# Hybrid decoder layer, one core: other places for the SBUF tiles, other orders of units and column groups, another source for the first norm

## Chip, cores and metric

One Trainium2 chip, one of its cores. The metric is the device time of one execution in microseconds (us), as a median over runs.

## What is computed

One decoder layer on 256 tokens of width 2048, in float32: a combined input projection that feeds eight gated-DeltaNet heads and eight block-sparse attention heads, an output projection, a cross-attention over 256 memory tokens, a gated MLP with a causal convolution, and a final norm. Cut to what matters here:

```python
def hybrid_mixer(x, ...):
    h = rmsnorm(x, norm_g)
    proj = h @ w_in                        # q, k, v, z, b, a | q, k, v  (7184 columns)
    qkv_a = silu(causal_dwconv(qkv_a, gdn_conv_w))
    o_a = rmsnorm(gated_delta_rule(...), gdn_norm_g) * silu(z_a)
    o_b = rmsnorm(moba_attention(q_b, k_b, v_b, rel_bias), moba_norm_g)
    return concatenate([o_a, o_b]) @ w_out

def cross_attention(x, mem, ...):          # 4 heads, keys and values from mem
def conv_ffn(x, ...):
    h = rmsnorm(x, norm_g)
    gate = causal_dwconv(h @ w_gate, conv_w) + conv_b
    return (silu(gate) * (h @ w_up)) @ w_down

x = x + hybrid_mixer(x); x = x + cross_attention(x, mem); x = x + conv_ffn(x)
return rmsnorm(x, final_norm_g)
```

## The kernel before, in words

**Numbers in two parts.** Each float32 operand of a large matmul is a sum of two float32r parts. `split` writes the tokens as `xT[:, k, :512]`: 256 columns of high part and 256 of low part for each of the 16 row tiles k. Each weight unit (128 x up to 1024 numbers) arrives by DMA in `raw`, ScalarE copies it to `hi`, and VectorE writes the remainder to `lo` (`prep`, which handles one unit). Three products are summed: high weight times both parts of the tokens, and low weight times the high part.

**Units and blocks.** Two units make a pair, which one DMA of SyncE's queue brings (`load_pair`); the ring has three `raw` tiles, four `hi` and four `lo`. `w_block` computes 128 output columns, transposed, from two units with eight row tiles each (`w_unit`): in a unit first eight matmuls with a `hi` slice as the stationary operand and the 512 columns of `xT[:, k]` as the moving one, and then eight with a `lo` slice and 256 columns. Both units of a block go hi, lo, hi, lo; the job that empties the block's PSUM bank is added after the last low matmul. There are 152 such blocks: 40 in the input projection, 4 memory keys, 16 of the output projection, 4 cross-attention queries and 88 gate and up blocks of the MLP. `s_block` does it the other way round: a slice of tokens (or of `actT`) is stationary and 256 to 512 columns of `hi` or `lo` move; for a row tile and a half of the tokens there are three matmuls (high by `hi`, low by `hi`, high by `lo`). The z gate, the values and the whole down projection (`actT`, 22 row tiles a half) are made so.

**Order.** `stream` issues the units in the order of the list `units`; between the parts of a unit `jobs.tick` issues steps of generators (evacuations, the recurrence, attention, norms) by a planner that keeps estimated engine times. The planner sets only the order in which each engine's instructions stand in its queue. The list begins with the 400 columns of the first z group (`z_pairs(0)`, whose first 16 columns are the decay inputs b and a), the first two row tiles in a unit each and the others two in a unit; then eight K blocks, after each of which comes one pair of the second and third z groups (384 and 256 columns); then Q, value, V, attention blocks, output projection, cross-attention, MLP.

**The start.** `start_job` splits the row tiles of `xraw`, the channel-major tokens, as they land; `load_x` loads them between the first weight pairs. After row tile 11 it also loads the tokens a second time, as they are in memory (`xn`, four DMAs of 512 KB on SyncE's queue), and sums their squares on ScalarE for the first norm's factor `r1`. `z_evac` and the jobs that need `r1` wait for it. Nine warm-up matmuls on `ones` run before the first data.

**Places in SBUF.** Tiles of a pool lie one behind the other in the order in which they are made, each rounded up to 32 bytes a partition; the pool `p0` begins at byte 16512. From the sizes in the code follow these starts in a partition: `cst` 16512, `sml` (338 floats), `ones`, `pw`, `raw` 20480, `hi` 45056, `lo` 61440, `xT` 77824, the small tiles `t` 110592, the three `pad`, `stats`, the four `tt` 130656, `relb`, then the tag E (`xraw`, later the bias tables and the residual) at 138880 and behind it the pool `pm` from 155264 (the heads' tiles AB, later `mT`; `oTm`, `oTg`, `oTx`). Modulo 512 that is 0 for `raw`, `hi`, `lo`, `xT` and `t`, 96 for `tt`, 128 for E and for every tile of `pm`. The pool `pf` of the MLP replaces `pm` and starts with a filler of 96 floats, so `actT` lies at 155648, 0 modulo 512.

## Time and profile before

| | us |
|---|---|
| median of 3 runs (lowest, highest) | 1337.7 (1336.53, 1338.1) |
| the profiled execution, its own time | 1335.58 |
| its span, first to last instruction | 1333.8 |
| TensorE busy in the span | 1318.6 (99%) |
| VectorE, ScalarE, GpSimd busy | 935.2, 692.3, 54.6 |
| mean granted TensorE clock | 0.998 of 2.4 GHz |
| moved by DMA | 250.43 MB, 188 GB/s on average |

TensorE's busy time is made of matmuls that overlap: one matmul's listed duration (some 390 ns for 512 columns) is from its start to its end in the pipeline, and the pace is read from start to start. So a stretch in which TensorE is busy throughout is judged by its length over the number of its matmuls.

### The profile page before, as it was taken

What the parts mean: (1) busy time and instruction counts of PE and PEld (TensorE: products, weight loads), DVE (VectorE), ACT (ScalarE), POOL (GpSimd) and SP (SyncE); (2) the same over time, 40 slices, a digit from 0 to 9 for tenths busy, and PEclk for the clock granted to TensorE, in tenths of its full rate; (3) what the DMA queues carried; (4) which work ended last, traced back from release to release, by engine and by line L of the source; (5) the groups of instructions that cost most, each with busy time, mean ns of one, the idle gap of its engine ahead of it and who ended that gap; (6) DMA issues with size and microseconds to landing.
All of it is one profiled execution on the core that took longest, in us unless ns stands there. A gap on an engine that the chain in (4) does not pass through costs nothing.

```text
span 1333.8 us, 19353 instructions
## 1 busy us (share of the span) xinstructions
PE 1318.6 (99%) x7414; PEld 1149.5 (86%) x7414; DVE 935.2 (70%) x1594; ACT 692.3 (52%) x1114; POOL 54.6 (4%) x140
## 2 busy tenths in 40 slices
PE   8999999999999999999999999999999999999997
PEld 8998888888788889998888888888888888888886
DVE  5688889867686766687777777545577777775554
ACT  5776555567564544565544445434344454444443
POOL 0101000202110000000000000000000000000000
PEclk9999999999999999999999999999999999999999
DMA  9665655624255655454545555555555555555552
GB/s 342 227 236 197 219 178 186 205 92 147 103 190 184 235 190 190 137 212 160 188 167 187 188 189 189 199 197 199 189 190 189 190 190 190 189 190 189 190 189 95
DMA packets 50793, 250.43 MB, mean 188 GB/s; under 512 B 11603, under 2 KB 15884, under 8 KB 23436
## 3 DMA queue, kind: packets, MB, share of 16 engines
q1 hardware_dynamic: 49152, 245.53, 51.6%
q0 software_dynamic: 448, 2.11, 0.5%
q10 hardware_dynamic: 1100, 1.54, 0.3%
q8 instruction: 58, 0.95, 0.3%
q14 instruction: 35, 0.29, 0.1%
HBM read 246.53 MB, written 2.64 MB: 187 GB/s over the span
## 4 chain that ended last, share of the span: by engine, by line
PE 68%; issue 0%; DVE 0%; ACT 0%; POOLq 0%; POOL 0%; ACTq 0%; DVEq 0%
PE bank L96 68%; ACT xn L96 0%; DVE tt L96 0%; DVE xT L96 0%; DVE xn L96 0%; POOLq L1462 0%; POOL stats L96 0%; DVE oTx L96 0%; DVE lo L96 0%; ACT oTx L96 0%; ACTq L96 0%; DVE xres L96 0%; DVE stats L96 0%; DVEq L96 0%
## 5 line engine op out<-in xcount | busy, mean ns | idle before, releaser
L96 DVE TENSOR_TENSOR lo<-raw,hi 128x1024 fp32r<-128x1024 f32 (+4 forms) x449 | 540.3, 1205 | 321.0 <-ACT hi L96 316.1
L96 ACT ACTIVATE hi<-raw 128x1024 fp32r<-128x1024 f32 (+4 forms) x449 | 466.8, 1041 | 431.4 <-PE bank L96 331.0
L96 PE MATMUL bank<-xT,hi 128*128 128x512 f32 x2112 | 542.9, 396 | 1.4 <-DVE xT L96 1.4
L96 PEld LDWEIGHTS bank<-xT,hi 128*128 128x128 f32 x2112 | 377.5, 189 | 70.4 <-issue 2.6
L96 PEld LDWEIGHTS bank<-xT,lo 128*128 128x128 f32 x2112 | 288.1, 190 | 20.0 <-issue 0.6
L96 PE MATMUL bank<-xT,lo 128*128 128x256 f32 x2112 | 301.1, 284 | 0.0
L96 PE MATMUL bank<-hi,actT 128*128 128x512 f32 x704 | 216.8, 389 | 0.0
L96 PEld LDWEIGHTS bank<-hi,actT 128*128 128x128 f32 x704 | 132.0, 188 | 27.2
L96 PE MATMUL bank<-lo,actT 128*128 128x512 f32 x352 | 136.9, 389 | 0.0
L96 PE MATMUL bank<-hi,xT 128*128 128x512 f32 (+3 forms) x320 | 86.1, 353 | 3.3 <-ACT xT L96 2.4
L96 DVE SCALAR_TENSOR_TENSOR t<-pad,sml,t 128x256 f32<-128x256 f32 x160 | 78.2, 489 | 7.8
L96 PEld LDWEIGHTS bank<-lo,actT 128*128 128x128 f32 x352 | 66.1, 188 | 13.8
L96 ACT ACTIVATE t<-bank 128x256 f32<-128x256 f32 (+1 forms) x164 | 56.8, 349 | 25.9 <-PE bank L96 25.9
L96 PEld LDWEIGHTS bank<-hi,xT 128*128 128x128 f32 x320 | 56.9, 190 | 8.8 <-ACT xT L96 3.2
L96 DVE TENSOR_TENSOR t<-bank,t 128x256 f32<-128x256 f32 x132 | 55.1, 417 | 9.7 <-ACT t L96 9.6
L96 PE MATMUL bank<-lo,xT 128*128 128x512 f32 (+3 forms) x160 | 55.9, 349 | 0.0
L96 POOL TENSOR_TENSOR stats<-stats,pw 128x2 f32<-128x2 f32 (+1 forms) x38 | 28.9, 761 | 564.0 <-DVE stats L96 564.0
L96 ACT ACTIVATE t<-t,sml 128x256 f32<-128x256 f32 x44 | 22.3, 506 | 39.6 <-DVE t L96 38.9
L96 DVE TENSOR_TENSOR t<-t,t 128x256 f32<-128x256 f32 x96 | 41.0, 428 | 2.0
L96 ACT ACTIVATE actT<-t 128x256 fp32r<-128x256 f32 x44 | 18.0, 413 | 46.6 <-DVE t L96 46.6
L96 PEld LDWEIGHTS bank<-lo,xT 128*128 128x128 f32 x160 | 30.3, 190 | 2.6
L96 PE MATMUL bank<-oTg,hi 128*128 128x512 f32 x128 | 32.4, 395 | 0.0
(157 smaller groups left out, 992.6 us busy)
## 6 DMA issues: line engine op xcount, KB each, us to landing
raw<-wst SPq DMA_DIRECT2D x212, 1024.0 KB, 4.8
raw<-wz SPq DMA_DIRECT2D x4, 768.0 KB, 4.1
raw<-wz SPq DMA_DIRECT2D x3, 800.0 KB, 8.3
xn<-x SPq DMA_DIRECT2D x4, 512.0 KB, 8.6
raw<-wz SPq DMA_DIRECT2D x4, 512.0 KB, 4.2
tt<-mem SPq DMA_DIRECT2D x8, 256.0 KB, 5.2
tt<-memT SPq DMA_DIRECT2D x8, 256.0 KB, 5.1
xres<-xT SPq DMA_DIRECT2D x4, 512.0 KB, 5.7
```

The costliest lines, as they stand in the source:

```text
L96: r = f(o, *a, **k)
```

## The change

It does five things.

- **Places.** `sml` loses the MLP's convolution numbers (162 floats instead of 338); they become a tile `smf` of `pf`, loaded by GpSimd's queue ahead of `fg`. `stats` has 516 floats instead of 640 (the scratch of `decay_job` is now in a `t` tile), a filler of 4 floats follows it, and `pf` has no filler.
- **Turned second units.** With `turn`, a unit goes low first and then high, and its last high matmul ends the block. All second units of input projection, cross-attention queries, gate and up blocks are turned, every other one of the memory keys, the output projection and the first four MLP blocks.
- **Interleaved column groups.** The first and second z groups are taken in turn, unit by unit: row tiles 0 to 3 one at a time (a unit each), the others two at a time. Each pair now holds the same row tiles of both groups, its token tiles are loaded just ahead of it (`x_with`), and the first two pairs are loaded in two parts. The third group's four pairs follow K blocks 0, 2, 4 and 6.
- **First norm.** `xn` and its four DMAs go. Squares are taken of `xraw` (eight ScalarE instructions of 512 columns), added up on VectorE, and summed over the channels by four one-column matmuls (`token_sums`).
- **Smaller orders.** The split of row tile 0 may be issued 0.6 us earlier by the planner's time; `natural_ss` issues its squares 5 us later by it; `kb_evac` waits for the recurrence's `U` only ahead of the value product; `out_norm` gets its scratch tile from its caller.

```diff
+Z1 = 4
 
 
 G_MIX, G_MEM, G_X, G_F = 0, 16, 32, 48
-G_GDN, G_MOBA, C_GDN, C_FFN, B_FFN = 64, 65, 66, 66 + 96, 66 + 96 + 132
-SMALL = B_FFN + FB
+G_GDN, G_MOBA, C_GDN = 64, 65, 66
+SMALL = C_GDN + 96
+
+C_FFN, B_FFN = 0, 132
+SMALL_F = B_FFN + FB
 
 K_ID, K_TRI, K_NEG, K_M32, K_X = 0, 128, 256, 384, 512
 CONST = 1024
-TW = 260
-FILL = 96
+TW, STATS = 260, 516
+FILL = 4
...
-    stats = p0.tile([P, 640], F32, name="stats")
+    stats = p0.tile([P, STATS], F32, name="stats")
+    p0.tile([P, FILL], F32, name="fill")
...
             ap, us = pairs[i]
-            n = sum(u.n for u in us)
-            for a, b in ((0, us[0].n), (us[0].n, n)) if i == 0 else ((0, n),):
+            if i < len(x_with):
+                load_x(*x_with[i])
+            for part in [us[:1], us[1:]] if i < 2 else [us]:
+                a, b = part[0].off, part[-1].off + part[-1].n
                 sp.dma_start(raw[i % NRAW][:, a:b], ap[:, a:b])
-                state[i] = state.get(i, sp.due)
+                for u in part:
+                    u.at = sp.due
             state["dma"] = i + 1
...
-    def w_unit(src, steps):
+    def w_unit(src, steps, turn=False):
+
 
         def high(lo_, hi_):
             def f(u):
@@ -302,11 +311,14 @@
                     if k == 0:
                         b["ps"] = now(acc)
                     ps, w, xk = b["ps"], slice(j * P, (j + 1) * P), src(k)
+                    last = turn and k == b["k"] - 1
                     if b["wide"]:
-                        mm(ps, u.hi[:, w], xk, start=k == 0, stop=False)
+                        mm(ps, u.hi[:, w], xk, start=k == 0, stop=last)
                     else:
                         mm(ps[:, :256], u.hi[:, w], xk[:, :256], start=k == 0, stop=False)
-                        mm(ps[:, :256], u.hi[:, w], xk[:, 256:], start=False, stop=False)
+                        mm(ps[:, :256], u.hi[:, w], xk[:, 256:], start=False, stop=last)
+                    if last:
+                        jobs.add(b["evac"](ps))
             return f
 
         def low(lo_, hi_):
@@ -314,17 +326,19 @@
                 for j in range(lo_, hi_):
                     b, k = steps[j]
                     last = k == b["k"] - 1
-                    mm(b["ps"][:, :256], u.lo[:, j * P:(j + 1) * P], src(k)[:, :256], start=False, stop=last)
-                    if last:
+                    mm(b["ps"][:, :256], u.lo[:, j * P:(j + 1) * P], src(k)[:, :256], start=False,
+                       stop=last and not turn)
+                    if last and not turn:
                         jobs.add(b["evac"](b["ps"]))
             return f
         n = len(steps)
         cuts = [0, (3 * n) // 8, (6 * n) // 8, n]
-        return Unit(n * P, [high(a, b) for a, b in zip(cuts, cuts[1:])] + [low(0, n // 2), low(n // 2, n)])
-
-    def w_block(src, evac, wide=True):
+        hs, ls = [high(a, b) for a, b in zip(cuts, cuts[1:])], [low(0, n // 2), low(n // 2, n)]
+        return Unit(n * P, ls + hs if turn else hs + ls)
+
+    def w_block(src, evac, wide=True, turn=True):
         b = {"k": KT, "wide": wide, "evac": evac}
-        return [w_unit(src, [(b, k) for k in range(i, i + 8)]) for i in (0, 8)]
+        return [w_unit(src, [(b, k) for k in range(i, i + 8)], turn and i > 0) for i in (0, 8)]
...
-            while ("qb", h) not in box or not done["bt"] or done["U"] < H:
+            while ("qb", h) not in box or not done["bt"]:
...
-            while h >= H // 2 and done["y"] < H:
-                yield
+            while done["U"] < H or (h >= H // 2 and done["y"] < H):
+                yield
+            t = yield from T.get()
...
+    def token_sums(ps, a):
+
+        for tb in range(2):
+            for i in range(2):
+                mm(ps[:, tb:tb + 1], a[:, i * 256 + tb * P:i * 256 + (tb + 1) * P], ones[:, :1],
+                   start=i == 0, stop=i == 1)
...
-            plan.cur.end = sp.due
+            plan.cur.end = sp.due + 5.0
...
-            w = sml[:, C_FFN + j * 3:C_FFN + j * 3 + 3]
+            w = box["smf"][:, C_FFN + j * 3:C_FFN + j * 3 + 3]
...
-            act.activation(a, a, AF.Silu, bias=gcol(B_FFN, j))
+            act.activation(a, a, AF.Silu, bias=box["smf"][:, B_FFN + j:B_FFN + j + 1])
...
-    def z_pairs(n):
-        us_ = s_block(xs(1), list(range(KT)), ZW[n], z_evac(n), first=0 if n else 2)
-        o, ps = KT * sum(ZW[:n]), []
+    def z_pairs(us_, o):
+        ps = []
         for i in range(0, len(us_), 2):
             w = sum(u.n for u in us_[i:i + 2])
             ps.append((wz[:, o:o + w], us_[i:i + 2]))
             o += w
         return ps
 
+    def z_units(n, first):
+        return s_block(xs(1), list(range(KT)), ZW[n], z_evac(n), first=first)
+
     def put(us):
         for i in range(0, len(us), 2):
             pair(wst[state.setdefault("w", 0)], us[i:i + 2])
             state["w"] += 1
 
-    for p_ in z_pairs(0):
+    for p_ in z_pairs([u for two in zip(z_units(0, Z1), z_units(1, Z1)) for u in two], 0):
         pair(*p_)
-    zp = z_pairs(1) + z_pairs(2)
+    zp = z_pairs(z_units(2, 0), KT * (ZW[0] + ZW[1]))
     for h in range(H):
         put(w_block(xs(1), k_evac(h)))
-        for p_ in zp[h:h + 1]:
+        for p_ in zp[h // 2:h // 2 + 1] if h % 2 == 0 else ():
...
-    b = [w_block(msrc, mk_evac(h)) for h in range(XH)]
+    b = [w_block(msrc, mk_evac(h), turn=h % 2 > 0) for h in range(XH)]
...
-    b = [w_block(osrc, resid_evac(n, 2, G_X, True)) for n in range(KT)]
+    b = [w_block(osrc, resid_evac(n, 2, G_X, True), turn=n % 2 > 0) for n in range(KT)]
...
-    g0, u0, g1, u1 = (w_block(xs(3), e(j)) for j, e in ((0, gate_evac), (0, up_evac), (1, gate_evac), (1, up_evac)))
+    g0, u0, g1, u1 = (w_block(xs(3), e(j), turn=e is up_evac)
+                      for j, e in ((0, gate_evac), (0, up_evac), (1, gate_evac), (1, up_evac)))
...
-    def load_x(n):
-        a, b = (1, 2) if n == 0 else (2 * n, 2 * n + 2)
-        sp.dma_start(xraw[:, a:b, :], ins["xT"][:, a:b, :])
-        xdue.extend([sp.due] * (b - a))
+    x_with = [(0, 1), (1, 2), (2, 3), (3, 4)] + [(k, k + 2) for k in range(4, KT, 2)]
+
+    def load_x(a, b):
+        if a:
+            sp.dma_start(xraw[:, a:b, :], ins["xT"][:, a:b, :])
+            xdue.extend([sp.due] * (b - a))
 
     for n in range(NRAW):
         load_pair()
-        load_x(n)
-    load_x(NRAW)
...
-            plan.cur.end = xdue[k]
+            while len(xdue) <= k:
+                yield
+            plan.cur.end = xdue[k] - (MARGIN if k == 0 else 0.0)
             yield
             split(xT[:, k, :], xraw[:, k, :] if k else first[:, :256], first[:, 256 + k:257 + k])
             box[1, k] = True
-            if k % 2 == 0 and k // 2 + NRAW + 1 < KT // 2:
-                load_x(k // 2 + NRAW + 1)
             if k == 3:
                 act.dma_start(cst, ins["cst"][:, :512])
                 act.dma_start(alb, bass.AP(tensor=ins["alb"].tensor, offset=ins["alb"].offset, ap=[[0, P], [1, 16]]))
             if k == 11:
                 act.dma_start(sml, ins["small"])
-                xn = pm.tile([P, 2, D], F32, tag="C", name="xn")
-                for n in range(4):
-                    c = slice(n * 512, (n + 1) * 512)
-                    sp.dma_start(xn[:, :, c], ins["x"].rearrange("(b p) d -> p b d", p=P)[:, :, c])
+            if k % 2:
+                t = yield from T5.get()
+                if k == 1:
+                    act.activation(t[:, :256], first[:, :256], AF.Square)
+                    act.activation(t[:, 256:], xraw[:, 1, :], AF.Square)
+                    sq = t
+                else:
+                    act.activation(t, xraw[:, k - 1:k + 1, :].rearrange("p b c -> p (b c)"), AF.Square)
+                    yield
+                    vec.tensor_tensor(sq, sq, t, op=OP.add)
+                    T5.put(t)
         T5.put(first)
-        s1 = stat(8)
-        plan.cur.end = sp.due
-        for n in range(4):
-            yield
-            for tb in range(2):
-                t = xn[:, tb, n * 512:(n + 1) * 512]
-                act.activation(t, t, AF.Square, accum_out=s1[:, tb * 4 + n:tb * 4 + n + 1])
-        yield
-        ss = stat(2)
-        vec.reduce_sum(ss, s1.rearrange("p (b n) -> p b n", b=2), axis=AX.X)
-        r1 = rstd_of(ss, D, 2)
+        yield
+        ps = yield from acc.get()
+        token_sums(ps, sq)
+        T5.put(sq)
+        yield
+        r1 = rstd_of(ps[:, :2], D, 2)
+        acc.put(ps)
...
-    pf.tile([P, FILL], F32, name="fill")
     box["actT"] = pf.tile([P, HB, 512], F32R, name="actT")
     fg = pf.tile([P, D], F32, name="fg")
+    box["smf"] = pf.tile([P, SMALL_F], F32, name="smf")
+    pool.dma_start(box["smf"], ins["smallf"])
...
-    wz = np.concatenate([c.reshape(KT, P, c.shape[1]).transpose(1, 0, 2).reshape(P, -1) for c in zc], axis=1)
+    zc = [c.reshape(KT, P, c.shape[1]).transpose(1, 0, 2) for c in zc]
+    ks = [(k, k + 1) for k in range(Z1)] + [(k, k + 2) for k in range(Z1, KT, 2)]
+    wz = [c[:, i:j].reshape(P, -1) for i, j in ks for c in zc[:2]] + [zc[2].reshape(P, -1)]
+    wz = np.concatenate(wz, axis=1)
```

## Rows read from the trace of the kernel before

**Rows 1.** the page: busy us of each engine, share of the span, instructions

```profile
PE 1318.6 (99%) x7414; PEld 1149.5 (86%) x7414; DVE 935.2 (70%) x1594; ACT 692.3 (52%) x1114; POOL 54.6 (4%) x140
```

**Rows 2.** whole stages, busy time by stretches: length, busy (instructions) by engine, clock, DMA, GB/s

```profile
419.03:508.96 89.93, 89.93 (x515) 78.49 (x513) 60.23 (x84) 43.38 (x54) 0.00 (x0) 1.00 0.57 207
840.18:959.88 119.70, 119.70 (x530) 99.14 (x529) 59.59 (x56) 47.10 (x48) 0.10 (x1) 1.00 0.54 193
959.88:1205.67 245.79, 245.79 (x1410) 216.31 (x1408) 183.46 (x284) 120.58 (x173) 1.89 (x19) 1.00 0.53 190
```

**Rows 3.** the same view: two stretches of the start

```profile
5.46:12.95 7.49, 4.32 (x16) 3.40 (x17) 3.71 (x8) 3.75 (x7) 0.00 (x0) 1.00 0.96 356
12.95:27.61 14.66, 14.66 (x82) 14.66 (x81) 12.74 (x20) 10.92 (x19) 0.00 (x0) 1.00 1.00 370
```

**Rows 4.** TensorE in order of time: start, us, what; gate and up, hi and xT at 0

```profile
703.30 2.00 PE L96 MATMUL bank<-xT,hi 128*128 128x512 f32 x8
705.14 1.12 PE L96 MATMUL bank<-xT,lo 128*128 128x256 f32 x8
706.10 2.00 PE L96 MATMUL bank<-xT,hi 128*128 128x512 f32 x8
```

**Rows 5.** the same view: output projection, hi at 0, oTm at 128

```profile
497.71 2.02 PE L96 MATMUL bank<-oTm,hi 128*128 128x512 f32 x8
499.57 1.10 PE L96 MATMUL bank<-oTm,lo 128*128 128x256 f32 x8
500.51 2.03 PE L96 MATMUL bank<-oTm,hi 128*128 128x512 f32 x8
502.38 1.12 PE L96 MATMUL bank<-oTm,lo 128*128 128x256 f32 x8
```

**Rows 6.** the same view: z group of 400 columns, every other row tile at 64

```profile
22.72 0.53 PE L96 MATMUL bank<-hi,xT 128*128 128x400 f32 x2
24.89 0.34 PE L96 MATMUL bank<-hi,xT 128*128 128x400 f32 x1
```

**Rows 7.** the same view at the start; in brackets idle time and what ended it

```profile
5.46 1.31 PE L96 MATMUL bank<-hi,xT 128*128 128x400 f32 x2
11.30 0.45 PE L96 MATMUL bank<-hi,xT 128*128 128x400 f32 x1 [2.45 <-ACT xT L96]
12.47 0.45 PE L96 MATMUL bank<-hi,xT 128*128 128x400 f32 x1 [0.72 <-DVE xT L96]
```

**Rows 8.** the same stretch on ScalarE

```profile
9.22 0.87 ACT L96 ACTIVATE hi<-raw 128x800 fp32r<-128x800 f32 x1 [3.42 <-DMA raw<-wz]
10.76 0.89 ACT L96 ACTIVATE xT<-xraw,tt 128x256 fp32r<-128x256 f32 x2
```

**Rows 9.** groups of 12 to 40 us: operation, shapes, count | busy us, mean ns | idle

```profile
L96 DVE SCALAR_TENSOR_TENSOR xT<-xraw,tt,xT 128x256 fp32r<-128x256 f32 x14 | 6.1, 478 | 0.0
L96 DVE TENSOR_TENSOR lo<-raw,hi 128x800 fp32r<-128x800 f32 x6 | 5.9, 987 | 0.2 <-ACT hi L96 0.2
L96 ACT ACTIVATE xT<-xraw,tt 128x256 fp32r<-128x256 f32 x12 | 5.4, 497 | 0.1
L96 ACT ACTIVATE hi<-raw 128x800 fp32r<-128x800 f32 x5 | 4.3, 864 | 0.7 <-DMA raw<-wz 0.7
```

**Rows 10.** the same groups view of the whole span: squares and their sum

```profile
L96 DVE TENSOR_TENSOR tt<-tt,tt 128x512 f32<-128x512 f32 x14 | 9.6, 685 | 0.0
L96 ACT ACTIVATE tt<-xres 128x512 f32<-128x512 f32 x16 | 9.9, 616 | 0.0
```

**Rows 11.** one-column sums as they stand in a later norm

```profile
516.79 0.95 PE L96 MATMUL bank<-ones,tt 128*128 128x1 f32 x8
517.60 0.49 PE L96 MATMUL bank<-hi,mT 128*128 128x256 f32 x2
```

**Rows 12.** GpSimd's load of fg; last row its landing

```profile
L96 POOL DMA_DIRECT2D fg<-fg x1: 627/627/627, 588.0 to 588.0; - x1
DMA to landing us min/median/max: 5.5/5.5/5.5
```

35 lines of the change are left out of this document (16 added, 19 removed).

## The prediction, made before the change was run

> **What bounds the kernel now.** Read the page's busy times first: TensorE is busy for 1318.6 of the span's 1333.8 us, VectorE 70%, ScalarE 52% [rows 1]. The next view is the busy time by stretches: in the large stages TensorE is busy to the last hundredth at full clock [rows 2], and the idle time that an edit could take back lies mostly at the start, where TensorE works 4.32 of 7.49 us [rows 3]. So the time is a sum of matmul paces, and the third view is the order of time, read from start to start. In the gate and up stage a run of eight 512-column matmuls lasts 1.84 us (703.30 to 705.14) and the eight 256-column ones behind it 0.96 [rows 4]; the whole stage has 88 units in 245.79 us, 2.793 us each [rows 2]. The first down half has 528 matmuls of 512 columns (22 row tiles x 2 halves of the tokens x 3 products x 4 column groups) in 119.70 us: 226.7 ns each [rows 2]. 512 columns at 2.4 GHz would be 213.3, so each pays 13.3 ns more. But the output projection, which issues the same instructions as the gate blocks, needs 89.93 us for 32 units, 2.810 each [rows 2], and its runs of eight take 1.86 and 1.87 us [rows 5]. The pace thus depends on something other than shape. What differs is the place: there the moving tile lies at 128 modulo 512 and the stationary one at 0; in the other two stages both lie at 0. That is my reading and the trace does not prove it.
>
> **Places, worked out.** `sml` shrinks from 1376 to 672 bytes a partition (rounded up to 32), so `raw`, `hi`, `lo`, `xT` and `t` move down by 704, from 0 to 320 modulo 512. `stats` takes 480 bytes less and the filler 32, so `tt` comes to 480 and E with all of `pm` and `pf` to 0. By this arithmetic the change doesn't do what its title says: the tiles that carry most matmuls leave the multiples of 512, and the others reach them. What counts then is whether the chip sees the place itself or the distance between the two operands. The distance of `hi` and `xT` stays 0; that of `hi` and the output projection's tiles goes from 128 to 192 (modulo 512, and 320 the other way round); that of `hi` and `actT` goes from 0 to 320. I take the distance: the runs in the output projection are uneven (1.86, 1.87, with stage mean above that of the gates), as two streams that get in each other's way would be, and a fixed toll for one tile's place should be even.
> *Down projection.* 1056 matmuls of 512 columns lose distance 0. Dear end: (1.86 + 1.87) / 16 = 233.1 ns against 226.7 [rows 2, 5], 6.4 x 1056 = 6.8 us. Cheap end: the 400-column z group, where every other row tile of `hi` lies at 64: its twelve matmuls from 22.72 to 24.89 take 2.17 us, 180.8 ns each [rows 6], where 400 columns and 13.3 ns would be 180.0; that is 1.7 ns for each displaced one, 1.8 us. Nothing excludes 0. I take +4.0, about halfway, as neither row has this distance.
> *Output projection.* Displaced before and after: 0, from -0.5 (32 x 17 ns, if it heals) to +0.5.
> The Trainium skill says in "TensorE: Matmul & The Clock Gate", Part 2, that the stationary and the moving operand come through two independent SBUF read ports, so that a weight load takes nothing from a running matmul; in "SBUF — State Buffer", "Who interferes with whom", that TensorE never waits on anyone. By this no place could matter. This case's 2.810 against 2.793 us for equal units speaks against it [rows 2]; the rule's outcome is rival A.
>
> **Turned units.** The first high run after low ones is slow: 1.84 us against 8 x 0.2267 = 1.813 in an unbroken run [rows 2, 4], 27 ns; the low run behind it shows nothing that large (0.96 for eight). A turned block has one such change instead of two, so up to 27 ns are saved a block. Blocks: 40 of the input projection, 4 queries, 84 of gate and up, and of the order in which units of four blocks alternate 2 + 8 + 2 changes: 140 x 27 ns = 3.8 us. In the first 40 small matmuls of other jobs break the runs, and some of the loss may come back in the low run; I take -2.6 (from -3.8 to -1.8, the 84 alone at four fifths). The bank is handed over at the same place, and `lo`, now first, is ready: preparation runs three units ahead, 8.4 us, against some 2.4 for its two instructions (864 and 987 ns for 800 columns, a unit here has 1024) [rows 9].
>
> **Start.** The second wait begins because the pair with row tiles 2 to 5 (800 KB) must land whole: ScalarE waits 3.42 us for it until 9.22, splits the tokens at 10.76, and TensorE idles until 11.30 and again until 12.47 [rows 7, 8]; in all 7.49 - 4.32 = 3.17 us [rows 3]. By 9.2, 136 + 200 + 200 + 128 + 800 = 1464 KB had to land. After the change row tile 1 of both groups needs 1048 KB, 1.2 us less at 356 GB/s: about 8.0, in `hi` at 8.5 and `lo` at 9.0 (half of 864 and 987 ns) [rows 9]. Row tile 0 of both groups, twelve matmuls from 5.46 on, occupies TensorE at least until 7.6, and longer, as the first two last 1.31 us to their end [rows 7]. So some 0.5 to 0.9 us of idleness remain. From there each row tile brings 520 KB, 1.46 us, for 12 matmuls or 2.12 us; the transfer is ahead. For two row tiles ScalarE has 864 + 843 + 2 x 497 + 616 = 3.3 us and VectorE 987 + 956 + 2 x 478 + 685 = 3.6 us, in 4.24 us [rows 9, 10] (843 and 956 are 768-column preparations, about 0.97 of the 800-column ones). The squares are in that sum, so they lie beside TensorE, but with 15% of cover. I take -2.8, the earlier split of row tile 0 included; from -1.0 (VectorE holds up the row tiles) to -3.8 (everything idle, and 0.6 from the split).
>
> **First norm.** The four 512 KB loads leave SyncE's queue, where weight pairs stood behind them, in a stretch with TensorE busy 14.66 of 14.66 us [rows 3]: 0. The four column sums are new: eight of a later norm take 0.81 us [rows 11]. Half of it and a broken run: +0.5. `r1` waits for row tile 15, four PSUM banks stay with the z groups until then, and K blocks fill the other four: 0 (to +1, if a K block finds no bank).
>
> **The rest.** `smf` goes on GpSimd's queue ahead of `fg`, whose issue at 588.0 and landing 5.5 us later [rows 12] put it at 594 or earlier; the first gate block ends with the stage's fifth unit, 5 x 2.79 us after the stage's start, near 602. Cover 8 us; if it were late, VectorE would stand with all preparation behind it. The job orders (`kb_evac`, `natural_ss`, `decay_job`) shift ScalarE and VectorE work, which have 30% and more to spare [rows 1]: 0, within 0.5. The third z group keeps its matmuls.
>
> **Sum.** -2.8 + 0.5 - 2.6 + 4.0 + 0 = -0.9. The profiled execution, 1335.58 (span 1333.8 and 1.8 around it), would become 1334.7; it lies 2.1 below the median, so the forecast for the median is 1337.7 - 0.9 = 1336.8. Its own range, by the bounds: 1332 to 1340.
>
> **Rivals.**
> A. *Places cost nothing* (or the tiles end where pace is not hurt). For it: the loss at 64 is under 1 ns in the mean [rows 6]. Against it: [rows 2, 5]. Then -2.8 + 0.5 - 2.6 = -4.9: 1332.8. An output projection that heals gives 0.5 more.
> B. *Each tile's own place counts.* Then `hi` and `xT` at 320 make every gate, up and input block as slow as the output projection's: 264 units (132 blocks) x 17 ns = 4.5 us, the down projection pays its 6.8, and turning gives nothing, as no run settles: -2.8 + 0.5 + 4.5 + 6.8 = +9.0: 1346.7. It decides as soon as a gate unit takes over 2.80 us. Against it: a displaced tile with 256 columns shows no loss (0.94 us for eight, against 0.96) [rows 4, 5].
> C. *The start gains little*, as VectorE's 3.6 of 4.24 us stand in a chain behind ScalarE: -1.0 instead of -2.8, 1338.6; it lies inside the main range.
>
> **How the numbers follow.** Main case 55% (C in it), A 25%, B 20%. About 0.2%, 2.7 us, is what a measurement of this kernel can tell from no change. The main case is over 2.7 faster in 24 of 100, within it in 71, slower in 5; A is faster in 90; B slower in 95. Faster: 0.13 + 0.23 = 0.36; slower: 0.03 + 0.19 = 0.22; the same: 0.42. The range from 1331 to 1344 holds the main case, most of A and a third of B.
>
> **What would show it.** Gate and up units in the order high 16, low 16 with the second stage at 244.8 us: turning and distance right; over 246, B. The down half at 121 to 123 us: the term of the places; at 119.7, A. The stretch from 5.46 to 12.95 with idleness under 1 us: the start; idle gaps behind VectorE there: C. The forecast is wrong if the unit pace changes anywhere but in the down projection, or if a job that was moved lets TensorE wait in the stages that are full now.

## The result and the profile after

The changed kernel takes 1350.02 us (median of four runs, 1349.9 to 1351.27); the kernel before, beside it, 1337.15. The ratio is 1.0098, with a 95% interval from 1.0086 to 1.0110. It is slower by 13 us, where 1336.8 and a range of 1331 to 1344 were predicted. The profiled execution has a span of 1348.1 us, 14.3 more than before.

The page after, its span and its busy times, answers to [rows 1]: TensorE works 3.9 us more in a span 14.3 us longer.

```profile
span 1348.1 us, 19376 instructions
...
PE 1322.5 (98%) x7422; PEld 1151.7 (85%) x7422; DVE 935.4 (69%) x1603; ACT 696.8 (52%) x1112; POOL 52.9 (4%) x141
```

So most of the loss is idle time that was not there before. The next view finds it: busy time by stretches (length, busy time and instructions of TensorE, its weight loads, VectorE, ScalarE and GpSimd, granted clock, DMA share, GB/s). The first two rows are the start, cut to the lengths of [rows 3]; then the memory keys, the output projection, the first down half and the second gate and up half, the last three as in [rows 2].

```profile
5.02:12.51 7.49, 7.49 (x40) 7.38 (x40) 5.03 (x11) 5.59 (x13) 0.00 (x0) 1.00 0.98 334
12.51:27.17 14.66, 12.66 (x70) 12.01 (x70) 11.62 (x19) 11.05 (x19) 0.00 (x0) 1.00 0.98 345
389.59:433.94 44.35, 33.25 (x169) 27.55 (x168) 26.79 (x68) 19.66 (x51) 5.49 (x10) 0.85 0.38 137
433.94:522.69 88.75, 88.75 (x513) 77.27 (x512) 59.58 (x83) 44.72 (x54) 0.00 (x0) 1.00 0.56 202
852.98:973.84 120.86, 120.86 (x530) 99.17 (x529) 59.38 (x55) 47.62 (x48) 0.10 (x1) 1.00 0.53 192
973.84:1218.77 244.93, 244.93 (x1410) 216.49 (x1408) 181.17 (x284) 121.83 (x173) 1.90 (x19) 1.00 0.53 189
```

The memory-key stage is the place. In the kernel before, the same stage, from its first matmul to the first of the output projection, was:

```profile
392.02:419.03 27.01, 26.05 (x158) 22.62 (x157) 21.79 (x51) 15.54 (x34) 5.44 (x7) 1.00 0.50 178
```

27.01 us have become 44.35, +17.3, and TensorE's idle time in them 11.1 us instead of 1.0. The rest is what the prediction argued about: output projection 88.75 against 89.93, down half 120.86 against 119.70, gate and up 244.93 against 245.79. Added up from first matmul to first matmul, the stages give -0.4 (start of the first), -2.0 (input), +17.3, -1.2 (output projection), +0.2 (queries and the memory values), -0.6 (second projection), -0.5 and -0.9 (gate and up), +1.2 and +1.2 (down): +14.3, the whole difference of the spans.

What TensorE waits for there, in the view of the waits of that stage (engine <- releaser: us in total, times, longest):

```profile
PE bank L100 <- DVE mT L100: 9.6, 5, 4.0
...
ACT mT L100 <- DMA tt<-memT: 5.4, 2, 4.6
DVE mT L100 <- ACT mT L100: 4.7, 2, 4.5
```

The normed memory `mT`, which this stage multiplies, comes late; ScalarE and VectorE, who write it, wait in turn for the load of `memT`. The kernel before has one such wait:

```profile
PE bank L96 <- DVE mT L96: 1.0, 1, 1.0
```

That row existed before the prediction. It says that `mT` can come after TensorE asks for it, and the prediction gave it no term. How much lateness still fits in, it doesn't say: below, `U` is 7 and 10 us later in two kernels that have no such wait.

Behind some of the waits the granted clock falls as well. Stretches of the same stage after:

```profile
398.32:402.50 4.18, 2.90 (x12) 2.49 (x13) 2.18 (x8) 2.84 (x8) 0.89 (x2) 0.58 0.01 2
402.50:416.50 14.00, 12.03 (x65) 10.26 (x64) 9.55 (x20) 7.02 (x15) 1.86 (x2) 0.88 0.33 115
416.50:422.30 5.80, 1.47 (x5) 0.68 (x5) 1.30 (x4) 1.04 (x3) 0.00 (x0) 0.75 0.91 350
422.30:427.00 4.70, 4.70 (x21) 4.40 (x22) 1.99 (x4) 1.44 (x2) 0.00 (x0) 0.58 0.17 65
```

The clock has two levels, 2.4 and 1.2 GHz (1.00 and 0.50 in this column), and a value in between is a stretch with some of each. Behind idle times of 2.04 and 1.28 us (ahead of 398.32 and 400.32) it is 0.58 on average; in 416.50 to 422.30 TensorE works 1.47 us of 5.80, and the next 4.70 us, though full, run at 0.58. Not every wait does that: the 2.45 us at the start of the kernel before [rows 7] are followed by a clock of 1.00 [rows 3]. Only slow clock under busy time costs anything. Taken from the means of these four stretches that is about 2.90 x 0.42 + 12.03 x 0.12 + 1.47 x 0.25 + 4.70 x 0.42 = 5.0 us, an estimate. So of the 17.3 us 10.1 are more waiting and 7.2 more busy time (33.25 - 26.05), some 5 of it slow clock; the other 2 weren't traced, and 11 more instructions stand in this stretch.

### The chain behind it

`mT` lies in the memory of `AB`, which the heads of the first attention hold to their end; the program issues the loads of `memT` only then. So the chain is: K blocks, triangular factors (stored to `lscr`), load into `sub`, 31 serial steps on VectorE, `U`, heads, `memT`, `mT`. The view by tile (count; ns least, median, most; first and last start in us) of the kernel before:

```profile
L96 SPq DMA_DIRECT2D sub<-lscr x2: 518/570/622, 142.8 to 143.4; - x2
L96 DVE TENSOR_TENSOR U<-U,bank x8: 414/418/422, 263.9 to 274.3; 128x256 f32<-128x256 f32 x8
L96 ACT ACTIVATE mT<-tt,sml x16: 492/501/513, 333.2 to 406.8; 128x256 fp32r<-128x256 f32 x16
```

and after:

```profile
L100 SPq DMA_DIRECT2D sub<-lscr x2: 511/546/582, 165.5 to 166.1; - x2
L100 DVE TENSOR_TENSOR U<-U,bank x8: 411/415/422, 294.8 to 309.0; 128x256 f32<-128x256 f32 x8
L100 ACT ACTIVATE mT<-tt,sml x16: 492/496/512, 362.0 to 421.6; 128x256 fp32r<-128x256 f32 x16
```

The load of `sub` is 22.7 us later, the last step of `U` 34.7 later (309.0 against 274.3), the last piece of `mT` 14.8 later. The chain begins later, too: the first matmul of the first K block, in order of time, before

```profile
27.61 1.56 PE L96 MATMUL bank<-xT,hi 128*128 128x512 f32 x6
```

and after:

```profile
42.33 1.55 PE L100 MATMUL bank<-xT,hi 128*128 128x512 f32 x6
```

At its end the chain runs through TensorE itself. From the view of the chain that ended last (start, us, what; SPq is SyncE's queue), ahead of the longest wait:

```profile
412.96 1.07 ACT hi L100
414.06 1.24 DVE lo L100
415.31 0.33 SPq L100
415.68 5.51 DMA tt<-memT
```

The last load of `memT` goes right behind another load on SyncE's queue, which began when VectorE had written `lo`; that followed ScalarE's `hi`, and that TensorE's matmuls up to there. So the date of the last `mT` also depends on the order in this queue, which no run here changed.

### The profile page after: what moved, and what is told of

It reads as the page before. It is cut to its first block, busy times and chain, and to the rows that moved or that the text cites. A ratio compares the mean times of both kernels' runs of the same rounds, so it can differ in the third digit from the quotient of the medians.

```text
span 1348.1 us, 19376 instructions
## 1 busy us (share of the span) xinstructions
PE 1322.5 (98%) x7422; PEld 1151.7 (85%) x7422; DVE 935.4 (69%) x1603; ACT 696.8 (52%) x1112; POOL 52.9 (4%) x141
## 3 DMA queue, kind: packets, MB, share of 16 engines
q10 hardware_dynamic: 1100, 1.45, 0.3%
## 4 chain that ended last, share of the span: by engine, by line
PE 95%; DMA 2%; ACT 1%; DVE 1%; issue 1%; SPq 0%; POOLq 0%; POOL 0%; ACTq 0%; DVEq 0%
PE bank L100 95%; DMA tt<-memT 1%; DMA raw<-wz 0%; DVE lo L100 0%; ACT hi L100 0%; DMA xraw<-xT 0%; ACT tt L100 0%; SPq L100 0%; ACT xn L100 0%; ACT L100 0%; DVE tt L100 0%; DVE mT L100 0%; ACT t L100 0%; DVE xT L100 0%; ACT mT L100 0%
## 5 line engine op out<-in xcount | busy, mean ns | idle before, releaser
L100 DVE TENSOR_TENSOR lo<-raw,hi 128x1024 fp32r<-128x1024 f32 (+3 forms) x452 | 539.1, 1195 | 336.2 <-ACT hi L100 328.5
L100 ACT ACTIVATE hi<-raw 128x1024 fp32r<-128x1024 f32 (+3 forms) x452 | 467.3, 1036 | 440.3 <-PE bank L100 397.0
L100 PE MATMUL bank<-xT,hi 128*128 128x512 f32 x2112 | 523.8, 394 | 1.4 <-DVE xT L100 1.4
L100 PEld LDWEIGHTS bank<-xT,hi 128*128 128x128 f32 x2112 | 383.7, 188 | 75.0 <-DVE xT L100 2.2
L100 PEld LDWEIGHTS bank<-xT,lo 128*128 128x128 f32 x2112 | 272.5, 191 | 12.0 <-issue 1.0
L100 PE MATMUL bank<-xT,lo 128*128 128x256 f32 x2112 | 281.7, 284 | 0.0
L100 PEld LDWEIGHTS bank<-lo,actT 128*128 128x128 f32 x352 | 66.1, 188 | 14.8
L100 DVE SCALAR_TENSOR_TENSOR t<-pad,smf,t 128x256 f32<-128x256 f32 x88 | 42.6, 485 | 6.1
L100 ACT ACTIVATE t<-t,smf 128x256 f32<-128x256 f32 x44 | 22.1, 501 | 40.0 <-DVE t L100 40.0
L100 DVE SCALAR_TENSOR_TENSOR t<-pad,sml,t 128x256 f32<-128x256 f32 x72 | 34.6, 483 | 3.2 <-ACT t L100 1.4
```

The lines of the kernel that those rows point to most:

```text
L100: r = f(o, *a, **k)
```

## Experiments

The trace shows where the time went, not which edit sent it there. The theory taken from it: interleaving puts the 384 columns of the second z group ahead of the first K block, so the chain starts some 15 us later and ends later. Rival causes: the job orders (logits computed ahead of `U`), the new first norm, the places.

### The old z order in the changed kernel, and two parts by themselves

Changed kernel with the old z order (excerpt):

```diff
-    for p_ in z_pairs([u for two in zip(z_units(0, Z1), z_units(1, Z1)) for u in two], 0):
+    for p_ in z_pairs(z_units(0, 2), 0):
...
-        for p_ in zp[h // 2:h // 2 + 1] if h % 2 == 0 else ():
+        for p_ in zp[h:h + 1]:
```

> The changed kernel with one part undone: the first two column groups of z run one after the other again, as before, with their old order of loads, and the second group's units stand between the K blocks again; the first norm from the channel-major tokens, the turned units, the job orders and all the places stay. Theory (the interleaving makes the K blocks start 10 to 15 us late, so the unit-triangular factors are late by 20, the serial substitution passes that on, and TensorE waits in the memory-key stage): the last factor is done near 140 instead of 160 us, the memory-key stage takes 27 to 30 us instead of 44, and the time is 1335 to 1339, that is 11 to 15 below the changed kernel. Rival 1 (the logits of the second attention are now computed ahead of the last substitution steps and take ScalarE, VectorE and the 512-column slots from them): the stage still takes about 44 us and the time is 1349 to 1352. Rival 2 (the norm of the tokens is late by 6 us, or the decay job holds one of the slots): the factors are still late by 5 to 10 us, and the time lies in the middle, 1341 to 1347.

Measured: 1340.35 us, 1.0022 (1.0012 to 1.0032). Undoing the interleaving gives back most of the loss, 9.7 us, but not all. The memory-key stage is back to 28.4 us. The factors come at 150.9, better than 160.4 and worse than the 140 expected: something besides the interleaving delays them. Neither the theory nor a rival came out whole. Part of what is left is the edit's own: it loads row tiles 2 to 5 in one transfer ahead of the second weight pair, where the kernel before loads two of them behind it, and TensorE's long wait at the start is 3.94 us instead of 2.45. The input stage is 3.8 us longer than before (390.4 against 386.6), the memory-key stage only 1.4.

Turned units alone, in the kernel before:

```diff
-        return Unit(n * P, [high(a, b) for a, b in zip(cuts, cuts[1:])] + [low(0, n // 2), low(n // 2, n)])
+        return Unit(n * P, ls + hs if turn else hs + ls)
```

> The kernel before with the turned second units alone (low products first, then high ones, evicted after the last high product). By the prediction's term (140 blocks at some 19 ns) 2.6 us are saved: the second stage of gate and up takes 244.9 us instead of 245.8, the time is 0.996 to 0.999 of before. Rival (the planner's changed dates shift the chain of the first attention): the memory-key stage grows by some us and the time rises by up to 5.

Measured: 0.9998 (0.9989 to 1.0008). The second gate and up half, busy time by stretches:

```profile
961.22:1206.15 244.93, 244.93 (x1409) 216.49 (x1408) 181.20 (x284) 121.90 (x173) 1.89 (x19) 1.00 0.53 189
```

As predicted, 0.86 less; the first half saves 0.6 (252.04 against 252.63). The ratio is above the 0.996 to 0.999 expected, as the memory-key stage is 1.0 longer and so is the start. The input stage as a whole gains nothing (386.9 against 386.6), but from the first K block to the memory keys it is 1.51 us shorter; before, and with turned units:

```profile
27.61:392.02 364.41, 364.41 (x2151) 316.99 (x2151) 287.00 (x625) 223.18 (x452) 41.45 (x80) 1.00 0.52 184
29.39:392.29 362.90, 362.90 (x2152) 316.86 (x2151) 286.19 (x628) 218.44 (x446) 40.69 (x83) 1.00 0.52 184
```

What hides it is the part ahead, 23.97 us instead of 22.15: the long wait there is 3.39 us instead of 2.45, and the clock 0.93 instead of 1.00. The edit doesn't touch that part, and the trace of the kernel before is that of an execution 2.1 us below its median; the runs with the places alone and the job orders alone have 0.93 there, too.

Places alone, in the kernel before (the fill tile stands for the smaller tables, the decay scratch goes into a slot):

```diff
+    p0.tile([P, 80], F32, name="fa")
...
-    stats = p0.tile([P, 640], F32, name="stats")
+    stats = p0.tile([P, 528], F32, name="stats")
...
-    pf.tile([P, FILL], F32, name="fill")
```

> The kernel before with the places of the changed one alone: raw, hi, lo, xT and the 256-column slots at 320 modulo 512, the 512-column slots at 480, E, the attention outputs and the activation tile at 0 (fill tiles stand for the smaller tables; the decay job's scratch lies in a 256-column slot). If only the distance between the stationary and the moving tile counts: each half of the down projection 1.1 to 1.4 us longer (120.9 instead of 119.7), the output projection 0.5 to 1.2 shorter, gate and up unchanged at 245.8; the time is 1.000 to 1.002 of before. If each tile's own place counted: every gate and up unit 17 ns longer, 1.005 to 1.008. If the places also had a part in the late chain of the first attention, the memory-key stage would be over 30 us long.

Measured: 0.9994 (0.9985 to 1.0004). Output projection, first down half, second gate and up half:

```profile
420.04:508.79 88.75, 88.75 (x514) 77.34 (x513) 60.15 (x84) 43.61 (x54) 0.00 (x0) 1.00 0.58 209
839.05:959.90 120.85, 120.85 (x530) 99.17 (x529) 59.55 (x56) 47.06 (x48) 0.10 (x1) 1.00 0.53 191
959.90:1205.71 245.81, 245.81 (x1409) 216.33 (x1408) 183.44 (x284) 120.57 (x173) 1.89 (x19) 1.00 0.53 190
```

-1.2, +1.15 and 0.0: the two stages whose distance changes move, the one whose two tiles move together doesn't. That is the distance; a toll for each tile's own place (rival B) is refuted.

### Pace by place

Each matmul has a weight load of its own; `W` lies at 0, the sixteen `x` at 0, 32, up to 480, `V` at 320:

```python
for x in X:
    run([(W, n, x, n, 512) for n in range(40)])
    run([(W, n, x, n, 256) for n in range(40)])
```

> A kernel of its own that leaves the whole layer out and only measures the pace of matmuls by place: one stationary tile at 0 modulo 512, moving tiles at 0, 32, up to 480, in runs of 40 with 512 and with 256 columns, each with a weight load of its own; then a stationary tile at 320 with moving tiles at 0, 128 and 320; then runs of 16 high products (both tiles at 0, 512 columns) and 16 low ones (stationary at each place, moving at 0, 256 columns). If the distance counts: 227 ns at distance 0 for 512 columns and 120 for 256; 229 to 234 and 113 to 114 at some other distances, moving minus stationary at 192 among them; the stationary tile at 320 gives with a moving one at 320 what 0 gives with 0. If a tile's own place counts: 320 with 320 differs from 0 with 0. If no place counts: one pace for each width, within 1 ns.

Busy time by stretches; each of the first six is 40 matmuls, each of the last four 16 (the count can take in a neighbour at the edge); the kernel was run once. In order: 512 columns at distances (moving minus stationary) 64 and 256, then 256 columns at distance 256; stationary at 320 with the moving tile at 0, first 512 and then 256 columns; both at 320, 512 columns; and runs of 16, high and low, with the low weights at 0 and then at 96.

```profile
46.91:56.06 9.15, 9.15 (x43) 7.51 (x41) 0.00 (x0) 0.00 (x0) 0.00 (x0) 1.00 0.01 2
131.09:140.17 9.08, 9.08 (x42) 7.51 (x41) 0.00 (x0) 0.00 (x0) 0.00 (x0) 1.00 0.01 2
140.17:144.96 4.79, 4.79 (x41) 4.79 (x40) 0.00 (x0) 0.00 (x0) 0.00 (x0) 1.00 0.00 0
243.15:252.49 9.34, 9.34 (x42) 7.49 (x41) 0.00 (x0) 0.00 (x0) 0.00 (x0) 1.00 0.01 2
252.49:257.04 4.55, 4.55 (x42) 4.55 (x41) 0.00 (x0) 0.00 (x0) 0.00 (x0) 1.00 0.00 0
270.74:279.83 9.09, 9.09 (x42) 7.51 (x41) 0.00 (x0) 0.00 (x0) 0.00 (x0) 1.00 0.01 2
284.62:288.28 3.66, 3.66 (x18) 3.01 (x17) 0.00 (x0) 0.00 (x0) 0.00 (x0) 1.00 0.00 0
288.28:290.19 1.91, 1.91 (x17) 1.90 (x16) 0.00 (x0) 0.00 (x0) 0.00 (x0) 1.00 0.00 0
317.99:321.64 3.65, 3.65 (x18) 3.01 (x17) 0.00 (x0) 0.00 (x0) 0.00 (x0) 1.00 0.00 0
321.64:323.52 1.88, 1.88 (x17) 1.87 (x16) 0.00 (x0) 0.00 (x0) 0.00 (x0) 1.00 0.00 0
```

Per matmul with 512 columns: 228.8 ns at 64, 227.0 at 256 (226.7 once the first few are through), 233.5 for 320 against 0, 227.3 for 320 against 320. The moving tiles at 256 to 480 repeat those at 0 to 224 to within 0.3 ns, so for 512 columns the pace follows the distance modulo 256, and of the eight distances only 0 reaches 226.7 (the others take 228.8 to 234.1). The down projection's stationary tile at 0 and its moving one at 320 are at distance 64 by that: 120.86 / 528 = 228.9 ns, which the 228.8 here foretells. With 256 columns the distance 0 is among the slow ones: 119.8 ns, against 113.8 for 320 against 0. In the runs of 16 the low products take 119.4 ns at 0 and 117.5 with their weights at 96, and the high ones between them don't pay for it (3.66 and 3.65 us). Here distance alone doesn't settle it: other tiles at the same distance gave 117.8 instead of 113.8, which stays open.

### Each remaining part alone

Interleaving with its loads; the first norm from the channel-major tokens; the job orders:

```diff
+    for p_ in z_pairs([u for two in zip(z_units(0, Z1), z_units(1, Z1)) for u in two], 0):
```

> The kernel before with the interleaved first two z groups alone (their order in the weights, the loads that go with it, no second-group units between the K blocks); old norm, no turned units, old job orders, old places. Theory 1 (the interleaving alone moves the K blocks back by 10 to 15 us, and the late chain of the first attention stops TensorE in the memory-key stage): the last unit-triangular factor is written at 152 to 160 instead of 140 us, the memory-key stage is 38 to 45 us long instead of 27, and the time is 1344 to 1350. Theory 2 (interleaving and the other job edits are needed together, as undoing it alone gave back 9.7 of 13 us with the factors still 11 us late): the factors come at 145 to 150, the memory-key stage takes 27 to 32 us and the time is 1335 to 1341.

```diff
+                    act.activation(t, xraw[:, k - 1:k + 1, :].rearrange("p b c -> p (b c)"), AF.Square)
+                    vec.tensor_tensor(sq, sq, t, op=OP.add)
...
+        token_sums(ps, sq)
```

> The kernel before with the first norm from the channel-major tokens alone (squares of the row-tile pairs, their running sum on VectorE, four one-column sums; the four 512 KB loads of the natural tokens fall away). By the prediction's terms: +0.5 for the sums, 0 for the loads: 1336.5 to 1338.5. Rival: the squares and the kept bank delay the first K units, the factors come 5 to 10 us later and the memory-key stage pays 3 to 8 us: 1340 to 1345.

```diff
-            while ("qb", h) not in box or not done["bt"] or done["U"] < H:
+            while ("qb", h) not in box or not done["bt"]:
...
-            while h >= H // 2 and done["y"] < H:
+            while done["U"] < H or (h >= H // 2 and done["y"] < H):
```

> The kernel before with the job orders alone: the logits of the second attention may be computed before the last substitution steps are through, its 256-column slot is taken later, the decay job's scratch lies in a 256-column slot, the norm's slot is handed on, natural tokens are dated 5 us later. By the prediction's term: 0, within 0.5, so 1336 to 1338. Rival: the logits take ScalarE, VectorE and slots from the substitution's tail and from the first attention's outputs; the last step of U then comes 5 to 14 us later after the factors than before (before: 134.1 us from factors to the last U; 148.6 in the changed kernel, 140.6 with the old z order), the memory-key stage gets 3 to 10 us longer, 1340 to 1347.

Measured: interleaving 0.9992 (0.9982 to 1.0002), norm 0.9981 (0.9971 to 0.9990), job orders 0.9984 (0.9975 to 0.9993). None of the five parts alone makes the kernel slower; two make it faster. The sum of the five deviations is -0.0051, and together they measure +0.0098. My theory 1 for the interleaving is wrong as it stood: its factors come at 152.3, 12 us late as expected, yet `U` is only 9.7 us late, and `mT` 12 us early:

```profile
L97 DVE TENSOR_TENSOR U<-U,bank x8: 411/420/423, 272.6 to 284.0; 128x256 f32<-128x256 f32 x8
L97 ACT ACTIVATE mT<-tt,sml x16: 491/501/512, 343.1 to 394.6; 128x256 fp32r<-128x256 f32 x16
```

```profile
395.03:420.24 25.21, 25.21 (x154) 22.31 (x153) 18.65 (x39) 12.99 (x28) 2.92 (x4) 1.00 0.47 172
```

The stage is full. (In this kernel a K block waits 2.26 us at 58 until a bank is emptied, the mishap that the prediction had priced at up to 1.) With the job orders alone, `U` is 7.2 us late and `mT` nevertheless 17 us early; I put that down to the logits, which the edit lets run ahead of `U`, but no run shows it:

```profile
L96 DVE TENSOR_TENSOR U<-U,bank x8: 411/412/421, 272.4 to 281.5; 128x256 f32<-128x256 f32 x8
L96 ACT ACTIVATE mT<-tt,sml x16: 489/497/513, 331.5 to 389.9; 128x256 fp32r<-128x256 f32 x16
```

So lateness has slack up to a point, and the parts may be harmless one by one and not together. In the kernels by then the last factor is late, against 140.2, by 12.1 (interleaving), 5.0 (norm), 1.9 (turning), 1.2 (places) and 0.8 us (jobs): 21.0 together, and the changed kernel's is at 160.4, 20.2 late. That the two agree so well is partly luck: in the traces of turning, places and job orders the first K block is already late, at 29.39, 28.82 and 28.86 us against 27.61, by the start's clock and wait, so these three latenesses aren't shown to come from the edits.

### Lateness by itself

To test this without any part that is under suspicion: kernel before, job orders of the change (they leave it 0.9984), and one date.

```diff
-        plan.cur.end = sp.due
+        plan.cur.end = sp.due + 27.0
         yield
         for r in range(31):
```

> The kernel before with the job orders and one number: the serial substitution may start 12 us later than its data land (nothing is added or left out, only its date is later; z order, norm, turning and places are those of before). Theory of the slack (each part of the change makes the first attention's chain a few us later; up to about 10 to 15 us this is hidden, beyond it TensorE waits in the memory-key stage): with the job orders alone the last step of U is at 281.5 us and that stage takes 25.5; 12 us later, near 293, it takes 26 to 30 and the time is 1335 to 1339. Rival (lateness has no slack, each us costs a us): 1346. Rival (lateness isn't the cause at all, but what the interleaving does to slots and banks): 1334 to 1336.

> As the run before with 27 instead of 12 us: the last step of U near 308, as in the changed kernel (309), with the old z order, norm, second units and places. Theory of the slack: the memory-key stage takes 40 to 46 us, TensorE idles about 10 us in it and runs part of it at half clock, the time is 1347 to 1353, as with the whole change. If the changed kernel's loss came from what the interleaving does to slots and banks and not from the date of U: the stage stays under 32 us and the time under 1340.

Measured: 12 us late 1.0030 (1.0020 to 1.0040), 27 us late 1.0097 (1.0082 to 1.0112). The second repeats the whole loss of the change, 1.0098, with none of its interleaving, norm, turning or places; its `U`, `mT` and memory-key stage:

```profile
L96 DVE TENSOR_TENSOR U<-U,bank x8: 411/414/422, 303.8 to 317.4; 128x256 f32<-128x256 f32 x8
L96 ACT ACTIVATE mT<-tt,sml x16: 491/497/539, 370.4 to 422.0; 128x256 fp32r<-128x256 f32 x16
```

```profile
388.01:432.81 44.80, 34.91 (x188) 28.05 (x187) 32.15 (x84) 22.79 (x61) 4.11 (x11) 0.92 0.41 146
```

9.9 us idle at a clock of 0.92. That the totals agree to 0.0001 is chance: its `U` is 8 us later than the changed kernel's, and its output projection (89.92) and second gate and up half (245.79) save nothing. The first costs more than I expected (1341.2 against 1335 to 1339): its `U` came at 297.6, not 293, and its last piece of `mT` at 413.7. Some of it is the start again: its input stage is 1.8 us longer than with the job orders alone (388.8 against 387.0). Both rivals are out for it: no slack at all would have given 1346, lateness without effect 1334 to 1336.

The other side of the test leaves both the interleaving and the norm out and keeps the rest; as edits of the kernel before:

```diff
-            while ("qb", h) not in box or not done["bt"] or done["U"] < H:
+            while ("qb", h) not in box or not done["bt"]:
...
+        return Unit(n * P, ls + hs if turn else hs + ls)
...
+    p0.tile([P, 80], F32, name="fa")
```

> Job orders, turned units and places together, without interleaving and without the new norm. Theory of the slack, with latenesses that add up: the last factor at 140.2 + 0.8 + 1.9 + 1.2 = 144.1 us, the last step of U at 274.3 + 7.2 + 2.5 + 1.2 = 285, the memory-key stage 25 to 28 us; by stages then (gate and up 1.4 less, output projection 1.2 less, down projections 2.4 more, memory keys 0 to 1.5 less) the time is 1334 to 1337. Rival (job orders and turned units or places hinder each other in some other way): over 1339.

Measured: 0.9970 (0.9960 to 0.9980), 1333.05 us, the memory-key stage full in 25.57 us. That is a little better than expected. The factors came at 141.2, not 144.1, with the first K block at 28.86 us: the 1.9 and 1.2 of turning and places were the start's and don't add.

All kernels by the chain's dates (start of the last one, us, for `mT` of VectorE's write of the low part, which follows ScalarE's; the two with low weights at 96 follow below; "to out" is from the first matmul of the input to the first of the output projection; "idle" is TensorE's in the memory-key stage):

| kernel | last factor | last `U` | last `mT` | to out | idle | ratio |
|---|---|---|---|---|---|---|
| before | 140.2 | 274.3 | 408.1 | 413.6 | 1.0 | 1 |
| jobs, turning, places | 141.2 | 280.8 | 388.1 | 411.9 | 0.0 | 0.9970 |
| jobs, turning, low weights at 96 | 141.5 | 280.7 | 387.8 | 411.4 | 0.0 | 0.9943 |
| turning, low weights at 96 | 141.2 | 275.2 | 407.7 | 413.5 | 2.2 | 0.9960 |
| jobs | 141.0 | 281.5 | 392.4 | 412.5 | 0.0 | 0.9984 |
| interleaving | 152.3 | 284.0 | 395.6 | 415.2 | 0.0 | 0.9992 |
| norm | 145.2 | 277.7 | 406.8 | 412.6 | 0.0 | 0.9981 |
| places | 141.4 | 275.5 | 409.2 | 414.8 | 1.0 | 0.9994 |
| turning | 142.1 | 276.8 | 409.2 | 414.9 | 1.7 | 0.9998 |
| all but interleaving | 150.9 | 291.5 | 411.9 | 418.8 | 1.8 | 1.0022 |
| jobs, 12 us late | 142.5 | 297.6 | 413.7 | 419.3 | 3.3 | 1.0030 |
| the whole change | 160.4 | 309.0 | 422.2 | 428.9 | 11.1 | 1.0098 |
| jobs, 27 us late | 141.1 | 317.4 | 422.6 | 427.6 | 9.9 | 1.0097 |

The idle time follows the last piece of `mT`: none up to 406.8, 1.0 to 3.3 us from 407.7 to 413.7, 10 to 11 at 422.

### Versions that are faster than both

The small kernel says what the low products' weights would gain from distance 96: 119.4 - 117.5 ns each. The change in the kernel before, with turned units, and the tables and scratch moved to make room:

```diff
+SHIFT = 24
...
-    lo = [p0.tile([P, 1024], F32R, name=f"lo{i}") for i in range(NRING)]
+    lo = [p0.tile([P, 1088], F32R, name=f"lo{i}") for i in range(NRING)]
...
+        h, ls = hi[i % NRING][:, :u.n], lo[i % NRING][:, u.shift:]
+        l = ls[:, :u.n]
```

> A candidate: the kernel before with the turned units and with the stationary tile of the low products displaced by 96 bytes against the moving one, in the units of whole blocks alone (hi, the moving tiles and the down projection's operands all stay at multiples of 256 bytes, the late bias and filter table is loaded with the activation tile, the decay scratch lies in a slot). The measurement by place gave 228.4 + 117.4 = 345.8 ns for a high and a low product in runs of 16 at this distance against 228.5 + 119.5 = 348.0 at distance 0. If that holds in the kernel: about 2200 low products by 2.2 ns, 4.8 us, and 1 us from turning: 1330 to 1333. If the low products reach the 113.4 ns of the changed kernel's output projection: 1320 to 1325. If the pace by place doesn't carry over from the small kernel: 1335 to 1337.

Measured: 1331.94 us, 0.9960 (0.9946 to 0.9975), as the first case has it. It still waits 2.2 us in the memory-key stage. With the job orders on top:

```diff
-            while ("qb", h) not in box or not done["bt"] or done["U"] < H:
+            while ("qb", h) not in box or not done["bt"]:
...
+        return Unit(n * P, ls + hs if turn else hs + ls, shift=SHIFT)
```

> A candidate: the turned units and the displaced low weights of the earlier candidate (1331.9, memory-key stage 28.4 us with 2.2 us of waits) with the job orders of the change. By the theory the last step of U comes near 282 us, inside the slack, and the job orders let the last piece of the normed memory come at 392 instead of 408 us, so that the memory-key stage takes 25.3 to 26: 2.5 to 3 us less, 1328.5 to 1330. If the two don't add: 1331 to 1333.

Measured: 1329.27 us, 0.9943 (0.9927 to 0.9960). Memory keys, then second gate and up half:

```profile
391.35:416.94 25.59, 25.59 (x157) 22.73 (x156) 17.83 (x37) 12.69 (x27) 1.77 (x4) 1.00 0.46 161
955.55:1199.01 243.46, 243.46 (x1409) 214.92 (x1408) 181.10 (x283) 121.82 (x173) 1.91 (x19) 1.00 0.53 190
```

No wait in the first, and gate and up 2.3 us shorter than before.

## Why the prediction was wrong

**The step that failed** stands under "The rest" and "First norm": the job orders shift work of engines "which have 30% and more to spare" and count 0, within 0.5 (alone they measured 2.3 us less); the K blocks wait for a bank at most, 0 to +1. Both priced a moved job by the load of an engine or a bank, and the date of the K blocks, which interleaving moves from 27.61 to 42.33, got no term at all. What the runs show in its place: the memory-key stage 17.3 us longer in the changed kernel, and the whole loss again (1.0097) from one date made 27 us later, with the job orders. An engine with 30% to spare says nothing on a chain that hands one result from engine to engine for 380 us. Lateness costs nothing at first (7 and 10 us in `U`, with the job orders or the interleaving alone); on top of the job orders 12 us then cost some 6 (0.9984 to 1.0030) and 27 us some 15 (to 1.0097). A sum of terms, each taken at the kernel before, could not show that. The other stages together give -3.0 us, which isn't far from the -0.9 forecast: this one stage made the miss. The last sentence of the prediction names the case (a moved job lets TensorE wait in a stage that is full now), without a term, a chance or a place.

**Start.** Forecast -2.8; measured -1.6: the first matmul 0.44 earlier, and 2.0 us idle instead of 3.17. The first 7.49 us are full, where 0.5 to 0.9 us of idleness were forecast. But row tiles 4 and 5 come in one piece again, and the wait returned there; ScalarE and then TensorE, after:

```profile
15.12 0.87 ACT L100 ACTIVATE hi<-raw 128x800 fp32r<-128x800 f32 x1 [3.18 <-DMA raw<-wz]
```

```profile
16.04 0.63 PE L100 MATMUL bank<-hi,xT 128*128 128x400 f32 x2 [1.60 <-ACT hi L100]
```

"The transfer is ahead" had been worked out for single row tiles only. Rival C, a chain on VectorE, isn't what happened: here ScalarE waits for the load.

**Turned units.** Mechanism and size about right: -2.6 forecast, with -1.8 for the 84 blocks of gate and up. Alone these gave -0.59 - 0.86 = -1.45 and the input, from its first K block on, -1.51. That is more than the 1.1 that 40 blocks at 27 ns could give, so part of it has another source that no run separates. The ratio of that part alone can't be told from 1.

**Places.** The arithmetic of the places holds, and the distance counts. Down projection: +4.0 forecast, from 0 to 6.8; +2.3 measured, which is 2.2 ns for each of 1056 matmuls, near the cheap end. The output projection: 0 forecast from -0.5 to +0.5; -1.2 measured, outside, since its 512-column products stay as slow (eight in 1.86 us from 511.60 to 513.46) while its 256-column ones fall from 117.5 ns between starts [rows 5] to 113.75 (sixteen from 513.46 to 515.28). Rivals A (places cost nothing) and B (own place) are both out. The Trainium skill's sentence in "TensorE: Matmul & The Clock Gate", Part 2, that a weight load takes nothing from the running matmul because the two operands have read ports of their own, would make every row of the small kernel the same for one width; the runs disagree, with 226.7 against 233.5 ns by the distance of the two tiles alone, and the measurement decides.

**First norm.** +0.5 for the sums was forecast; alone it is faster by 2.4 us (1334.78 against 1337.14), and its profiled execution, 1.1 us shorter, shows that it takes the wait out of the memory-key stage (25.83 us, full). The factors come 5.0 us later, 1.3 of them already at the first K block (28.93), and that stays hidden.

**Left open.** Between the last factor and the last `U` another 14.5 us are lost in the changed kernel (148.6 against 134.1). 6.4 are those of the job orders alone (140.5). The other 8 come with lateness alone: in the run that is 27 us late the way is 176.3, 8.8 more than 140.5 + 27, and in the one 12 us late 2.6 more, with the old z order and norm in both. What `U` meets when it is late stays open; that it is the logits and the heads on VectorE is only my argument. The changed kernel with the old order of the logits alone wasn't tried, nor interleaving and job orders without the new norm.

## What to carry to other kernels

Before a moved step is priced at zero because its engine has time to spare, write down the dates of the longest chain that passes through it, down to the first engine that waits for its end; a wait of 1.0 us there is a sign to look, whatever the busy shares say. The slack itself is measured by making one date later on purpose, as here by 12 and 27 us. Measure parts alone and then in pairs: interleaving, norm and job orders, harmless one by one, spent the same slack together. Where operands stream from two tiles, the distance of their starts modulo 256 bytes is worth a small kernel of its own, as the pace isn't one of shape alone: the distance read there gave 5 us (0.9960, against 0.9998 for turning alone), while tiles put at certain multiples gave none.

## What the runs showed of the hardware

The pace of matmuls with a weight load each depends on the distance between the two tiles: with 512 columns, where it follows the distance modulo 256 bytes, 226.7 ns at 0, 228.8 at 64 and 232 to 234 elsewhere; with 256 columns 119.8 at 0 and 113.3 to 120 elsewhere, depending on more than the distance. In the small kernel's runs of 16 the first five 512-column products after 256-column ones take, for instance, 233, 235, 229, 232 and 231 ns before they settle at 227, some 27 ns in all; a turned block has one such change less. And waiting can cost more than its length: in the memory-key stage of the changed kernel 10.1 us more of waiting came with stretches at a granted clock of 0.58, another 5 us or so, while a wait of 2.45 us in the start of the kernel before left the clock at 1.00.
